# Two norm rows moved inside a fp32 encoder-block kernel: the memory's row into the next projection, and the first token half's norm in two parts

## The chip, the cores and the metric

The kernel runs on one core of one Trainium2 chip. The metric is device time in microseconds. The kernel before takes 880.38 us, the median of 3 runs (880.06 to 880.5).

The engines are called as in the profile: PE is the matrix engine (PEld its weight loads), DVE the vector engine, ACT the scalar engine, POOL the general one, and SP the queue that issues most transfers.

## The reference

One layer of a hybrid encoder block on 512 tokens of width 1024, in fp32, with 256 memory tokens:

```
h = rms_norm(x);  proj = h @ w_in          # mLSTM q,k,v,o,gates | NA q,k,v | memory q | merge gates
y_ml = bidirectional mLSTM(...)            # chunks of 64, 4 heads of 128
y_na = 2-D neighbourhood attention(...)    # 8 heads of 64, window 8 x 16
mem_k, mem_v = split(rms_norm(mem) @ w_mem_kv)
y_xa = cross attention(xa_q, mem_k, mem_v) # 4 heads of 128
merged = g_ml*(y_ml@w_br_ml) + g_na*(y_na@w_br_na) + g_xa*(y_xa@w_br_xa)
x = x + merged @ w_out
x = x + (gelu(conv3(a)) * u) @ w_down      # a, u = split(rms_norm(x) @ w_up), width 2816 each
return rms_norm(x)                         # y = x * rsqrt(mean(x*x) + eps) * g
```

Two of the four norms matter here: that of the memory, and the last one, over the finished x.

## The kernel before

**Layout.** Activations are kept transposed: 128 features on the partitions, the 512 tokens along the free axis, eight such tiles for a width of 1024. Each fp32 operand is split into a high and a low fp32r part, and each product is three fp32r matmuls (`mm3`, L213 to L215): high by high, high by low, low by high. Weights stream from memory; each block of 1024 columns is split on arrival by ACT (L195) and DVE (L196).

**Norms.** The gain is folded into the split, and the reciprocal root is applied to the product. It is needed in two shapes, a column (one value for each token, tokens on the partitions) and a row (the value of each token in every partition). Three helpers make them:

- `two_parts` (L294) splits the sum of squares over feature tiles into a high and a low fp32r tile, one ACT copy (L296) and one DVE subtraction (L297).
- `rstd_cols` (L300) sums over partitions with two fp32r matmuls against a matrix of ones (L305), picks the diagonal with a DVE reduction against the identity (L309, one for each 128 tokens, and a read of its accumulator), and raises to the power -0.5 on POOL (L312).
- `rstd_row` (L315) splits the column into high and low (ACT L319, DVE L320), multiplies the identity by each value (DVE L325, one for each 128 tokens and part) to get diagonals, spreads them with two fp32r matmuls against ones (L326), and copies the result out (ACT L328).

**Order.** Each engine works through its instructions in the order of the program; the tile framework adds the semaphore waits. A projection `proj` is 24 matmuls, and a caller can hang work between its steps with `at={k: f}`. A generator holds the mLSTM and attention work, and `step()` puts a piece of it between projections; `tc.issue_after` keeps an instruction behind a named one.

**The memory's norm.** The squares of the memory are summed during the projections for its queries. In the loop over the four "o" projections (L980 to L994) the column is made after f = 1 and the row after f = 2, as a whole: diagonals and matmuls one behind the other. The row is first read at L999, after the first key projection.

**The end of the kernel** (`last_tiles`, L1111). The last down projection adds to x. Tokens 0 to 255, the first half, are finished in the transposed layout: `half_tile` makes features 640 to 1023 for them in three tiles (`f` = 5, 6, 7), and adds their squares to the sum `acc3`. Then comes one more half tile, f = 5 for the second half of tokens. The first half's last norm is made under it: after its step 5 `cols_a` runs, two fp32 matmuls of one column (L1138), mean and eps on DVE (L1140), the power on POOL (`power`, L1108), and two diagonals on DVE (L1144); after its last step `row_a` runs, one fp32 matmul against ones (L1148) and an ACT copy (L1150). Then eight DVE multiplications (`scale_a`, L1154) scale the first half, and two transfers (`store_a`, L1157) write it out.

Tokens 256 to 511 are finished the other way round, in two rounds of 128 tokens (t = 2 and t = 3): tokens on the partitions, eleven steps `k` of three matmuls each, and between them transposes of finished features (`turn`, L1173). In round 2, at step 3 and at step 4, `sums` (L1174 to L1180) sums `acc3` over partitions for these tokens by a matmul (L1177) and scales on DVE (L1179). From the second of these a value for round 3 is worked out (L1197) and written into column 256 of round 3's own accumulator bank; the first matmul of round 3 waits for that write. At the end of each round come the square sum of its own 256 columns, a power, the scaling and the stores.

Of the kernel before, what the change touches and what calls it, by code (L numbers as in the profile page):

```python
# [11 lines left out]
F32 = mybir.dt.float32  # L12
F32R = mybir.dt.float32r
AF = mybir.ActivationFunctionType
ALU = mybir.AluOpType
AX = mybir.AxisListType

P = 128
# [92 lines left out]
def hybrid_block(ctx, tc, xg, xT, memT, wflat, vecs, gbias, nabias, outa, outb):  # L111
# [18 lines left out]
    def unit(dt=F32):  # L130
        return up.tile([P, UNIT], dt, tag="unit", name=nm("u"))
# [10 lines left out]
    def atps():  # L142
        return atp.tile([P, 512], F32, tag="at", name=nm("at"))
# [156 lines left out]
    def rstd_cols(parts, ntok, tag, n=D):  # L300

        nt = ntok // P
        ps = atps()
        for i in range(2):
            st["mm"] = PE.matmul(ps[:, :ntok], onesr, parts[i], start=i == 0, stop=i == 1).ins  # L305

        v, junk = tiny(nt), scr(P)
        for t in range(nt):
            V.tensor_tensor_reduce(junk, ps[:, t * P:(t + 1) * P], ident, 1.0 / n, EPS, ALU.mult, ALU.add,  # L309
                                   accum_out=v[:, t:t + 1])  # L310
        col = cp.tile([P, nt], F32, name=f"rc_{tag}")
        st["pool"] = G.tensor_tensor(col, v, nhalf[:, :nt], op=ALU.pow).ins  # L312
        return col

    def rstd_row(col, ntok, tag):  # L315

        nt = ntok // P
        ch, cl = tp.tile([P, 32], F32R, tag="tiny", name=nm("y"), bufs=12)[:, :nt], tiny(nt)
        A.activation(ch, col, AF.Copy)  # L319
        V.tensor_tensor(cl, col, ch.bitcast(F32), op=ALU.subtract)  # L320
        pb = atps()
        for n, c in enumerate((ch.bitcast(F32), cl)):
            dg = sp.tile([P, S], F32R, tag="scr", name=nm("s"))[:, :ntok]
            for t in range(nt):
                V.tensor_scalar(dg[:, t * P:(t + 1) * P], ident, c[:, t:t + 1], None, op0=ALU.mult)  # L325
            PE.matmul(pb[:, :ntok], onesr, dg, start=n == 0, stop=n == 1)  # L326
        rb = cp.tile([P, ntok], F32, name=f"rb_{tag}", tag=f"rb{ntok}", bufs=1)
        A.activation(rb, pb[:, :ntok], AF.Copy)  # L328
        return rb
# [42 lines left out]
    def proj(key, XHs, XLs, n=S, bank=None, at={}):  # L372
        ws = weights(key)
        ps = (bank or mmps)()
        for k in range(KT):
            mm3(ps[:, :n], ws[k][0], ws[k][1], XHs[k], XLs[k], k == 0, k == KT - 1)
            if k == 1:
                flush()
            if k in at:
                at[k]()  # L380
        return ps
# [576 lines left out]
    def step(n=1):  # L958
        quota[0] += n
        while quota[0] >= 1 and gens:  # L960
            try:
                next(gens[0])
                quota[0] -= 1
            except StopIteration:
                gens.pop(0)
        if not gens:
            quota[0] = 0.0
# [3 lines left out]
    gens.append(ml_all())  # L971

    xq = unit()
    for f in range(4):
        ps = proj(("xaq", f), XH, XL)
        V.tensor_tensor(xq[:, f * S:(f + 1) * S], ps, rb, op=ALU.mult)
        mem_part(f)
        step(RB)
    for f in range(4):
        ps = proj(("o", f), XH, XL)  # L980
        t = scr()
        V.tensor_tensor(t, ps, rb, op=ALU.mult)
        A.activation(t, t, AF.Tanh, scale=0.5)
        if f == 0:
            so.append(unit())
            msum = two_parts(macc, M)
        if f == 1:

            with tc.issue_after(st["mm"]):
                mrc = rstd_cols(msum, M, "m")  # L990
        if f == 2:
            mrb = rstd_row(mrc, M, "m")
        V.tensor_scalar(so[0][:, f * S:(f + 1) * S], t, 1.0, None, op0=ALU.add)
        step(RB)  # L994
    mkv = unit()
    mk, mv = mkv[:, 0:1024], mkv[:, 1024:2048]
    for f in range(4):
# [113 lines left out]
    def last_tiles(U, UL_):  # L1111
# [20 lines left out]
        for f in range(LF - 1, KT):  # L1132
            half_tile(f, slice(0, Hf))

        def cols_a():
            ps = atps()
            for t in range(2):
                PE.matmul(ps[:, t:t + 1], acc3[:, t * P:(t + 1) * P], ones[:, 0:1], start=True, stop=True)  # L1138
            v = tiny(2)
            V.tensor_scalar(v, ps[:, :2], 1.0 / D, EPS, op0=ALU.mult, op1=ALU.add)  # L1140
            col = power(v)
            half["d"] = scr(Hf)
            for t in range(2):
                V.tensor_scalar(half["d"][:, t * P:(t + 1) * P], ident, col[:, t:t + 1], None, op0=ALU.mult)  # L1144

        def row_a():
            pb = atps()
            PE.matmul(pb[:, :Hf], ones, half["d"], start=True, stop=True)  # L1148
            half["r"] = scr(Hf)
            A.activation(half["r"], pb[:, :Hf], AF.Copy)  # L1150

        def scale_a(eng, *tiles):
            for i in tiles:
# [2 lines left out]
        def store_a(i):  # L1156
            SY.dma_start(outa[i * P:(i + 4) * P, :].rearrange("(f p) s -> p f s", p=P), x2v[i // 4][:, :, :Hf])  # L1157

        half_tile(LF - 1, slice(Hf, S), {5: cols_a, HF - 1: row_a})
        for i in (0, 4):  # L1160
            scale_a(V, *range(i, i + 4))
            store_a(i)
        banks = [mmps(), mmps()]
        for t in range(2, NT):
            tsl, osl = slice(t * P, (t + 1) * P), slice((t - 2) * P, (t - 1) * P)
            last = t == NT - 1
            bank = banks[t - 2]
            ps = bank[:, :256]
            pts = [atps(), mmps()]
            r = scr(256)  # L1170

            def turn(i):
                PE.transpose(pts[i // 4][:, i % 4 * P:(i % 4 + 1) * P], x2[i][:, tsl], ident)  # L1173

            def sums(sl):
                pc = atps()
                PE.matmul(pc[:, :1], acc3[:, sl], ones[:, 0:1], start=True, stop=True)  # L1177
                v0 = tiny(1)
                V.tensor_scalar(v0, pc[:, :1], 1.0 / D, EPS, op0=ALU.mult, op1=ALU.add)  # L1179
                return v0  # L1180

            for k in range(HF):
                mm3(ps, U[k][:, tsl], UL_[k][:, tsl], ws[k][0], ws[k][1], k == 0, k == HF - 1)
                if k == 1 and last:

                    for i in range(LF, KT):
                        PE.matmul(ps[:, (i - LF) * P:(i - LF + 1) * P], x2[i][:, tsl], ident, start=False, stop=False)
                elif k == 1:
                    for i in range(LF, KT):
                        turn(i)  # L1190
                    A.activation(r, pts[1][:, 256:], AF.Copy)
                if not last and k == 3:
                    v0 = sums(tsl)
                if not last and k == 4:

                    v1 = sums(slice(S - P, S))
                    V.scalar_tensor_tensor(banks[1][:, 256:257], v1, D ** 0.5, power(v1), op0=ALU.mult, op1=ALU.mult)  # L1197
                if not last and k == HF - 3:
                    for i in range(LF):
                        turn(i)  # L1200
            if last:
                for i in range(LF):
                    turn(i)
            sq, v = scr(257), tiny(1)
            if last:
                oa, ob = scr(), scr()

                A.activation(sq, bank[:, :257], AF.Square, scale=D ** -0.5, accum_out=v)
                A.activation(oa[:, 256:], pts[0][:, 256:], AF.Copy)
                col = power(v)  # L1210
                A.activation(oa[:, :256], pts[0][:, :256], AF.Copy, scale=col)
                first = V.tensor_scalar(oa[:, 256:], oa[:, 256:], col, None, op0=ALU.mult).ins
                SY.dma_start(outb[osl, :512], oa)

                with tc.issue_after(first):
                    V.scalar_tensor_tensor(ob[:, 256:], ps, col, gfin, op0=ALU.mult, op1=ALU.mult)
                A.activation(ob[:, :256], pts[1][:, :256], AF.Copy, scale=col)
                A.dma_start(outb[osl, 512:], ob)
                continue
            V.tensor_tensor(r, ps, r, op=ALU.add)  # L1220
            ss = tiny(1)
            A.activation(sq[:, :256], r, AF.Square, accum_out=ss)
            V.tensor_scalar(v, ss, 1.0 / D, v0, op0=ALU.mult, op1=ALU.add)
            col = power(v)
            o = unit()
            V.scalar_tensor_tensor(o[:, 768:1024], r, col, gfin, op0=ALU.mult, op1=ALU.mult)
            SY.dma_start(outb[osl, 768:], o[:, 768:1024])
            A.activation(o[:, :512], pts[0], AF.Copy, scale=col)
            SY.dma_start(outb[osl, :512], o[:, :512])
            A.activation(o[:, 512:768], pts[1][:, :256], AF.Copy, scale=col)  # L1230
            SY.dma_start(outb[osl, 512:768], o[:, 512:768])
# [162 lines left out]
```

## Time and profile before

| | |
|---|---|
| median of 3 runs | 880.38 us (880.06 to 880.5) |
| the profiled execution's own time | 880.21 us |
| its span | 878.4 us |
| PE busy | 873.1 us, 99% of the span |
| DVE, ACT, POOL busy | 580.5, 453.4, 126.9 us |
| memory row made (L319 to L328) | from 135.5 to 140.0 us |
| last half tile and first half's norm | from 858.6 to 864.0 us |
| rounds t = 2 and t = 3 on PE | from 863.2 to 873.8 us |

A row of a timeline has the start in us, the length in us, the engine, the line, the operation, its output and input tiles with their shapes, how many instructions are merged into it, and in brackets how long the engine sat idle before and what ended that. The length of a matmul is the time until its result stands; the next one starts earlier, so the distance between starts is what one costs PE. A fp32 matmul (not fp32r) shows as two records.

### The profile page before, as it was taken

Reading aid. Unit: us, or ns where it says so; the run is one execution under the profiler, and the core shown is the slowest. Engines: PE = TensorE matmul, PEld = TensorE weight load, DVE = VectorE, ACT = ScalarE, POOL = GpSimd, SP = SyncE. Lnnn points to the kernel's source line nnn. Section 1 sums busy time; section 2 is a strip of 40 time slices with the busy share of each in tenths; the row PEclk is TensorE's granted clock in tenths of the full one; section 3 lists DMA queues with packets and bytes.
Section 4 is the critical chain, followed back from the end, with each engine's and each line's share of the span. In section 5 each row is a group of like instructions: output and inputs, shape, how many; then the busy total and the mean of one; then the engine's idle time right before and its main releaser. Section 6 shows DMA issues by size and latency. Waiting matters only on the chain.

```text
span 878.4 us, 12253 instructions
## 1 busy us (share of the span) xinstructions
PE 873.1 (99%) x4338; PEld 740.0 (84%) x4338; DVE 580.5 (66%) x1206; ACT 453.4 (52%) x955; POOL 126.9 (14%) x203
## 2 busy tenths in 40 slices
PE   9999999999999999999999999999999999999997
PEld 7898889888888888888888888888888888888897
DVE  7694687766577758898676558776633466666433
ACT  7363556654556658888544435444422344444532
POOL 0101100000072460700000002111100011111011
PEclk9999999999999999999999999999999999999999
DMA  7224643522242353533223422222233322222412
GB/s 274 99 73 145 203 133 121 169 93 87 84 121 87 107 159 118 156 110 130 97 97 109 144 107 94 99 97 96 74 101 104 107 96 98 97 98 85 141 34 96
DMA packets 39293, 99.68 MB, mean 113 GB/s; under 512 B 5688, under 2 KB 13752, under 8 KB 39232
## 3 DMA queue, kind: packets, MB, share of 16 engines
q1 hardware_dynamic: 31440, 92.19, 30.6%
q0 software_dynamic: 7360, 6.32, 3.2%
q8 instruction: 34, 0.56, 0.3%
q10 hardware_dynamic: 432, 0.39, 0.1%
q14 instruction: 27, 0.22, 0.1%
HBM read 94.67 MB, written 4.21 MB: 113 GB/s over the span
## 4 chain that ended last, share of the span: by engine, by line
PE 99%; issue 0%; ACT 0%; DVE 0%; POOLq 0%; POOL 0%; DVEq 0%
PE mm L215 29%; PE mm L213 29%; PE mm L214 29%; PE at L214 2%; PE at L213 2%; PE at L215 2%; PE at L832 1%; PE at L686 1%; PE at L813 1%; PE at L651 1%; PE at L688 1%; PE at L794 0%; PE at L795 0%; PE at L667 0%; PE at L920 0%
## 5 line engine op out<-in xcount | busy, mean ns | idle before, releaser
L213 PE MATMUL mm<-u,wh 128*128 128x512 f32 (+1 forms) x1076 | 416.8, 388 | 0.0
L215 PE MATMUL mm<-u,wl 128*128 128x512 f32 (+1 forms) x1076 | 413.6, 384 | 0.0
L214 PE MATMUL mm<-u,wh 128*128 128x512 f32 (+1 forms) x1076 | 413.4, 384 | 0.0
L195 ACT ACTIVATE wh<-wr 128x512 fp32r<-128x512 f32 (+3 forms) x299 | 185.2, 622 | 246.7 <-PE mm L214 193.3
L196 DVE TENSOR_TENSOR wl<-wr,wh 128x512 fp32r<-128x512 f32 (+3 forms) x300 | 202.9, 678 | 91.5 <-ACT wh L195 86.9
L215 PEld LDWEIGHTS mm<-u,wl 128*128 128x128 f32 x1076 | 202.2, 188 | 40.7 <-DVE wl L196 0.6
L214 PEld LDWEIGHTS mm<-u,wh 128*128 128x128 f32 x1076 | 202.4, 188 | 39.1 <-DVE u L220 0.3
L213 PEld LDWEIGHTS mm<-u,wh 128*128 128x128 f32 x1076 | 202.4, 188 | 38.6 <-ACT wh L195 0.3
L1263 POOL TENSOR_TENSOR s<-s,rb 128x512 f32<-128x512 f32 x22 | 38.3, 1739 | 250.0 <-DVE s L1262 241.9
L499 POOL DMA_DIRECT2D u<-nav_d x128 | 62.2, 518 | 64.3 <-PE at L832 22.5
L219 ACT ACTIVATE u<-s 128x512 fp32r<-128x512 f32 x26 | 16.4, 631 | 56.3 <-DVE s L1266 56.1
L1266 DVE TENSOR_TENSOR s<-mm,s 128x512 f32<-128x512 f32 x22 | 15.2, 691 | 25.1 <-POOL s L1263 25.1
L419 ACT ACTIVATE s<-pad,vec 128x512 f32<-128x512 f32 x30 | 24.4, 812 | 9.2 <-DVE pad L417 9.2
L420 DVE SCALAR_TENSOR_TENSOR s<-pad,vec,s 128x512 f32<-128x512 f32 x30 | 23.6, 785 | 5.9 <-ACT s L419 5.8
L220 DVE SCALAR_TENSOR_TENSOR u<-s,u 128x512 fp32r<-128x512 f32 x26 | 18.0, 691 | 14.3 <-ACT u L219 14.1
L1262 DVE SCALAR_TENSOR_TENSOR s<-s,s 128x512 f32<-128x512 f32 x22 | 15.2, 692 | 13.4 <-ACT s L1261 13.3
L312 POOL TENSOR_TENSOR rc<-y,nhalf 128x4 f32<-128x4 f32 x1 | 1.0, 1032 | 152.5 <-DVE y L309 152.5
L421 DVE SCALAR_TENSOR_TENSOR s<-pad,vec,s 128x512 f32<-128x512 f32 x30 | 22.5, 750 | 0.8
L1261 ACT ACTIVATE s<-s 128x512 f32<-128x512 f32 x22 | 13.9, 631 | 15.1 <-DVE s L1260 15.1
L417 DVE TENSOR_TENSOR pad<-mm,rb 128x512 f32<-128x512 f32 x22 | 15.1, 690 | 7.3 <-PE mm L215 6.6
L1045 DVE TENSOR_TENSOR s<-mm,rb_x 128x512 f32<-128x512 f32 x16 | 11.0, 688 | 12.6 <-PE mm L215 12.6
L213 PE MATMUL mm<-wh,u 128*128 128x512 f32 x48 | 19.0, 396 | 0.0
(301 smaller groups left out, 1030.7 us busy)
## 6 DMA issues: line engine op xcount, KB each, us to landing
wr<-wflat SPq DMA_DIRECT2D x141, 512.0 KB, 3.2
nab<-nabias SPq DMA_DIRECT2D x16, 256.0 KB, 2.6
u<-nav_d POOLq DMA_DIRECT2D x128, 32.0 KB, 2.7
s<-xT SPq DMA_DIRECT2D x15, 256.0 KB, 3.7
wr<-wflat SPq DMA_DIRECT2D x14, 192.0 KB, 2.3
nav_d<-nv POOLq DMA_DIRECT2D x8, 256.0 KB, 2.7
R<-rd SPq DMA_DIRECT2D x8, 256.0 KB, 3.8
wr<-wflat SPq DMA_DIRECT2D x2, 544.0 KB, 3.2
```

What stands on the lines that cost most here:

```text
L195: A.activation(h[:, u:v], src, AF.Copy)
L196: V.tensor_tensor(l[:, u:v], src, h[:, u:v].bitcast(F32), op=ALU.subtract)
L213: PE.matmul(ps, lh, rh, start=start, stop=False)
L214: PE.matmul(ps, lh, rl, start=False, stop=False)
L215: st["mm"] = PE.matmul(ps, ll, rh, start=False, stop=stop).ins
L219: A.activation(h, src, AF.Copy, scale=scale)
L220: V.scalar_tensor_tensor(l, src, scale, h.bitcast(F32), op0=ALU.mult, op1=ALU.subtract)
L419: A.activation(t1, pad[:, 0:512], AF.Identity, scale=vcol(w, i), bias=vcol(b, i))
L420: V.scalar_tensor_tensor(t1, pad[:, 1:513], vcol(w, n + i), t1, op0=ALU.mult, op1=ALU.add)
L421: V.scalar_tensor_tensor(t1, pad[:, 2:514], vcol(w, 2 * n + i), t1, op0=ALU.mult, op1=ALU.add)
L499: G.dma_start(vw[r * 32:(r + 1) * 32, i * 256:(i + 1) * 256], nav_v[hf, r, CW[b]:CW[b] + 32, hp * 256:(hp + 1) * 256])
L1263: G.tensor_tensor(c, c, rb2, op=ALU.mult)
```

## The change

1. `rstd_row` is cut in two. `row_parts` makes both diagonals; `rstd_row` then issues the two matmuls and the copy, from given diagonals or from those that it makes.
2. For the memory the diagonals are made where the whole row was made before, after the "o" projection f = 2. The two matmuls and the copy are issued within the next projection, f = 3, after its step 1.
3. For the first half of tokens the fp32 norm is replaced by the general helpers: `two_parts` of `acc3` ahead of the last half tile, `rstd_cols` and `row_parts` after its step 6 (before: step 5), and the row's matmuls and copy after step 2 of round t = 2 (before: after the half tile's last step). The eight scalings and the two stores go with the row, so they come after step 2 of round 2 too. So the second half tile's addition to x (L1126) stands behind `row_parts` on DVE, and the scalings stand behind the first scaling of `sums` and ahead of the second one on DVE.

```diff
-        col = cp.tile([P, nt], F32, name=f"rc_{tag}")
+        col = tiny(nt) if tag == "a" else cp.tile([P, nt], F32, name=f"rc_{tag}")
...
-    def rstd_row(col, ntok, tag):
+    def row_parts(col, ntok):
         nt = ntok // P
         ch, cl = tp.tile([P, 32], F32R, tag="tiny", name=nm("y"), bufs=12)[:, :nt], tiny(nt)
         A.activation(ch, col, AF.Copy)
         V.tensor_tensor(cl, col, ch.bitcast(F32), op=ALU.subtract)
-        pb = atps()
-        for n, c in enumerate((ch.bitcast(F32), cl)):
+        dgs = []
+        for c in (ch.bitcast(F32), cl):
             dg = sp.tile([P, S], F32R, tag="scr", name=nm("s"))[:, :ntok]
             for t in range(nt):
                 V.tensor_scalar(dg[:, t * P:(t + 1) * P], ident, c[:, t:t + 1], None, op0=ALU.mult)
+            dgs.append(dg)
+        return dgs
+
+    def rstd_row(col, ntok, tag, parts=None):
+        dgs = parts or row_parts(col, ntok)
+        pb = atps()
+        for n, dg in enumerate(dgs):
             PE.matmul(pb[:, :ntok], onesr, dg, start=n == 0, stop=n == 1)
...
-        ps = proj(("o", f), XH, XL)
+        def mem_row():
+            with tc.issue_after(st["mm"]):
+                mrbs.append(rstd_row(mrc, M, "m", mparts))
+
+        ps = proj(("o", f), XH, XL, at={1: mem_row} if f == 3 else {})
...
         if f == 2:
-            mrb = rstd_row(mrc, M, "m")
+            mparts = row_parts(mrc, M)
...
+        asum = two_parts(acc3[:, :Hf], Hf)
+
         def cols_a():
-            ps = atps()
-            for t in range(2):
-                PE.matmul(ps[:, t:t + 1], acc3[:, t * P:(t + 1) * P], ones[:, 0:1], start=True, stop=True)
-            v = tiny(2)
-            V.tensor_scalar(v, ps[:, :2], 1.0 / D, EPS, op0=ALU.mult, op1=ALU.add)
-            col = power(v)
-            half["d"] = scr(Hf)
-            for t in range(2):
-                V.tensor_scalar(half["d"][:, t * P:(t + 1) * P], ident, col[:, t:t + 1], None, op0=ALU.mult)
-
-        def row_a():
-            pb = atps()
-            PE.matmul(pb[:, :Hf], ones, half["d"], start=True, stop=True)
-            half["r"] = scr(Hf)
-            A.activation(half["r"], pb[:, :Hf], AF.Copy)
+            half["c"] = rstd_cols(asum, Hf, "a")
+            half["p"] = row_parts(half["c"], Hf)
...
-        half_tile(LF - 1, slice(Hf, S), {5: cols_a, HF - 1: row_a})
-        for i in (0, 4):
-            scale_a(V, *range(i, i + 4))
-            store_a(i)
+        half_tile(LF - 1, slice(Hf, S), {6: cols_a})
...
+                if not last and k == 2:
+                    with tc.issue_after(st["mm"]):
+                        half["r"] = rstd_row(half["c"], Hf, "a", half["p"])
+                    for i in (0, 4):
+                        scale_a(V, *range(i, i + 4))
+                        store_a(i)
                 if not last and k == 3:
                     v0 = sums(tsl)
```

More of the change, by code (lines that the diff above doesn't have):

```diff
@@ L973, in hybrid_block @@
     xq = unit()
+    mrbs = []
     for f in range(4):
@@ L991, in hybrid_block @@
         if f == 2:
-            mrb = rstd_row(mrc, M, "m")
+            mparts = row_parts(mrc, M)
         V.tensor_scalar(so[0][:, f * S:(f + 1) * S], t, 1.0, None, op0=ALU.add)
         step(RB)
+    mrb = mrbs[0]
     mkv = unit()
```

## The prediction

> **What bounds the kernel.** I read the clock row and the chain that ended last first, then the timelines of PE, DVE, ACT and POOL over the last 20 us, since both parts of the change lie in the order of a few instructions.
>
> ```profile
> PEclk9999999999999999999999999999999999999999
> ```
> ```profile
> PE 99%; issue 0%; ACT 0%; DVE 0%; POOLq 0%; POOL 0%; DVEq 0%
> ```
>
> PE is the chain from end to end, at full clock. So each change counts by what it puts on PE or takes off it, and by the time that PE waits. A microsecond of DVE or ACT counts only where PE waits for it. The profiled execution took 880.21 us, 0.17 us less than the median of 880.38; I work out differences against its trace and add them to the median.
>
> The end of the kernel on PE, then DVE, ACT, POOL and the store queue at the same time:
>
> ```profile
> 860.60 0.28 PE L215 MATMUL mm<-u,wl 128*128 128x256 f32 x1
> ...
> 861.28 0.28 PE L214 MATMUL mm<-u,wh 128*128 128x256 f32 x1
> ...
> 862.83 0.28 PE L215 MATMUL mm<-u,wl 128*128 128x256 f32 x1
> ...
> 863.50 0.28 PE L214 MATMUL mm<-u,u 128*128 128x256 f32 x1
> ...
> 865.02 0.30 PE L1177 MATMUL at<-ones,acc 128*128 128x1 f32 x2
> ...
> 868.64 0.28 PE L213 MATMUL mm<-u,u 128*128 128x256 f32 x1
> ```
> ```profile
> 863.15 0.42 DVE L1126 TENSOR_TENSOR u<-mm,u 128x256 f32<-128x256 f32 x1 [0.44 <-PE mm L215]
> 864.07 0.43 DVE L1154 TENSOR_TENSOR u<-u,s 128x256 f32<-128x256 f32 x1 [0.49 <-ACT s L1150]
> 864.41 0.42 DVE L1129 TENSOR_TENSOR acc<-acc,s 128x256 f32<-128x256 f32 x1
> 864.74 2.43 DVE L1154 TENSOR_TENSOR u<-u,s 128x256 f32<-128x256 f32 x7
> 867.09 0.21 DVE L1179 TENSOR_SCALAR y<-at 128x1 f32<-128x1 f32 x2
> 867.97 0.17 DVE L1197 SCALAR_TENSOR_TENSOR mm<-y,y 128x1 f32<-128x1 f32 x1 [0.66 <-POOL y L1108]
> ```
> ```profile
> 859.66 0.51 ACT L1130 ACTIVATE u<-u,vec 128x256 f32<-128x256 f32 x1
> 863.65 0.38 ACT L1150 ACTIVATE s<-at 128x256 f32<-128x256 f32 x1 [3.47 <-PE at L1148]
> 863.93 0.41 ACT L1128 ACTIVATE s<-u 128x256 f32<-128x256 f32 x1
> 864.37 0.51 ACT L1130 ACTIVATE u<-u,vec 128x256 f32<-128x256 f32 x1
> 864.79 0.36 ACT L1191 ACTIVATE s<-mm 128x256 f32<-128x256 f32 x1
> ```
> ```profile
> 861.49 0.70 POOL L1108 TENSOR_TENSOR y<-y,nhalf 128x2 f32<-128x2 f32 x1 [11.67 <-DVE y L1140]
> 867.38 0.55 POOL L1108 TENSOR_TENSOR y<-y,nhalf 128x1 f32<-128x1 f32 x1 [5.19 <-DVE y L1179]
> ```
> ```profile
> 865.90 1.80 SPq L1157 DMA_DIRECT2D outa<-u  x2
> 871.30 0.34 SPq L1227 DMA_DIRECT2D outb<-u  x1
> ```
>
> See three things. PE has no gap here. The sum of the second half (DVE L1129) ends at 864.83, just ahead of the matmul that reads it (865.02). And the write that round 3 waits for (L1197) ends at 868.14, only 0.50 ahead of round 3's first matmul (868.64). So DVE has little to spare at two places, and the change queues more work on DVE ahead of both.
>
> **The memory's row.** Moved are two fp32r matmuls and a copy; the ACT copy, the DVE subtraction and the four diagonals stay where they were. No transfer moves.
>
> ```profile
> 130.60 0.40 PE L305 MATMUL at<-s,onesr 128*128 128x256 f32 x2
> 130.84 0.39 PE L667 MATMUL at<-u,u 128*128 128x128 f32 x2
> ```
> ```profile
> 138.55 0.40 PE L214 MATMUL mm<-u,wh 128*128 128x512 f32 x1
> ...
> 139.38 0.40 PE L215 MATMUL mm<-u,wl 128*128 128x512 f32 x1
> ```
>
> Two matmuls of 256 columns cost 0.24 (130.60 to 130.84), 0.12 each. Between L214 and L215 from 138.55 on lie the row's two matmuls and, between them, one fp32 matmul of the mLSTM, of 128 columns (half of the 0.43 that one of 256 costs below, 0.22). From 0.83 go an ordinary step of 0.23 (two of 256 columns), the 0.24 and the 0.22: 0.14 is lost, to the wait for the diagonals and to changing between fp32 and fp32r. In the changed order the fp32 matmul stands with its like, and the row comes four matmuls later (0.9 us), behind its diagonals. I take -0.15, between 0.1 (the new place breaks up a stream of fp32r) and -0.25. The row is first read after the first key projection; a copy that is a microsecond later meets nobody.
>
> **The last norm: PE's work.** Removed are the one-column fp32 sums and the fp32 row: 861.28 less 860.60 is 0.68, where two ordinary steps take 0.24, so 0.44; 863.50 less 862.83 is 0.67, so 0.43. Added are four fp32r matmuls of 256 columns, 0.48. Net -0.39. Two of the last four transposes now stand ahead of round 3 (0.22); at the end they saved nothing, as ACT waited for the last sum there, not for them.
>
> **The last norm: PE's first wait.** All DVE work up to the diagonals now stands ahead of the addition L1126, and L1126 leads to the sum that PE reads at step 3 of round 2. The helper's rows, from the norms of x, whose form is the same for twice the tokens:
>
> ```profile
> 28.25 0.61 PE L305 MATMUL at<-s,onesr 128*128 128x512 f32 x2
> ```
> ```profile
> 29.45 0.29 DVE L309 CUSTOM_DVE_ANT_0 s<-at,ident 128x128 f32<-128x128 f32 x1 [1.23 <-PE at L305]
> ```
> ```profile
> 30.83 1.03 POOL L312 TENSOR_TENSOR rc_x<-y,nhalf 128x4 f32<-128x4 f32 x1 [28.29 <-DVE y L309]
> ```
> ```profile
> 132.33 0.88 POOL L312 TENSOR_TENSOR rc_m<-y,nhalf 128x2 f32<-128x2 f32 x1 [17.42 <-DVE y L309]
> ```
> ```profile
> 523.74 0.21 ACT L319 ACTIVATE y<-rc 128x4 fp32r<-128x4 f32 x1 [2.42 <-POOL rc L312]
> ```
> ```profile
> 523.98 0.16 DVE L320 TENSOR_TENSOR y<-rc,y 128x4 f32<-128x4 f32 x1 [1.39 <-ACT y L319]
> 524.06 1.26 DVE L325 TENSOR_SCALAR s<-ident,y 128x128 fp32r<-128x128 f32 x6
> ```
>
> - Split of `acc3`: ACT is free at 860.15 (859.66 + 0.51), copy 0.38 and subtraction 0.42 with handoffs of 0.04: ready at 861.0. PE: without the old sums, step 6 runs from 860.72 to 861.08 and the two sums start at 861.08 and 861.20. Nothing waits; the last result stands at 861.48 (0.28 long).
> - Reduction: four tiles took 1.38 from first start to POOL, so two take 0.71 (0.33 each and the handoff). Its start: the row of x shows 0.59 from PE's last result (28.86) to 29.45 with DVE idle. All other handoffs from PE to an idle DVE are near 0.04 (862.83 + 0.28 to 863.15). I take 0.04, since that one was the first use of the instruction and had a separate wait in front of it, and keep 0.59 as the other end: 861.52, POOL at 862.23.
> - Power of two columns: 0.70 with DVE idle, 0.88 with DVE busy; DVE is idle here, so 0.70: 862.93. High and low part: ACT and DVE, 0.24 to the subtraction and 0.08 to the first diagonal: 863.26. Diagonals start 0.20 apart: the high pair is ready at 863.74, the low one at 864.13.
> - PE: round 2 starts at 862.76, two steps, two transposes (0.22), step 2 until 864.06. The row's matmuls then find their diagonals and end at 864.30. Step 3 ends at 864.66.
> - L1126 follows the diagonals on DVE, at 864.04 instead of 863.15, though its input stood at about 862.9. Then 0.42 and 0.04, ACT's square 0.41 and 0.04, DVE's addition 0.42: 865.37. PE's sum follows at 865.45: it waits 0.76 from 864.66.
>
> **PE's second wait.** On ACT the square (864.50), L1191's copy, the scaling and the row's copy follow each other at the old distances: 864.94, 865.24, 865.66, ended 866.04. The eight scalings start at 866.08, 0.336 apart (864.74 to 867.09 for seven), and end at 868.77. Only then come the second scaling of `sums`, POOL and the write: 0.99 from the start of that scaling (867.15) to the end of the write (868.14). So the write ends at 869.76, and round 3 starts at 869.80. PE itself would be there at 865.45 + 3.62 (865.02 to 868.64) + 0.22 for the two transposes, 869.29; it waits another 0.51.
>
> Here a page speaks for more. The Trainium skill, "VectorE: DVE Perf Modes", section "The DRAIN you can't avoid", says that the next vector instruction does not start until the pipe is empty; eight scalings of 0.43 would then take 3.44 and put the total 0.75 higher, near 882.1. The row of these very instructions, at this size, shows starts 0.336 apart, so the row decides and the rule gets no chance of its own.
>
> The two stores move with the scalings, by some 1.6 to 2 us on SP: the next store in that queue is issued at 871.30, so their cover is over 3 us and they cost nothing; without it they would cost what they are late.
>
> **Sum.** Round 3 starts at 869.80 instead of 868.64: +1.16. (By parts: waits 0.76 and 0.51, transposes 0.22, work -0.39, together 1.10; the rest is rounding.) Round 3 and what follows it are unchanged, and the other work of round 2's end, later by as much, has over 1 us before ACT is needed again. With the memory's -0.15 it is +1.0: 881.4 us.
>
> **Rivals.**
> 1. The reduction starts late (0.59), perhaps with the slow power (0.88) too: the whole chain moves by 0.55 to 0.73, and both waits with it: 881.9 to 882.2.
> 2. No wait binds, because the framework's order or shorter handoffs let L1126 and the write through in time: only work counts, -0.39 and -0.15: 879.8. Against it: on DVE L1126 stands in program order behind the diagonals, and the scalings ahead of the write. If only the second wait is covered, +0.76 - 0.39 - 0.15, 880.6.
> 3. Slower for certain: PE's clock steps down in the new waits. Round 3 has 33 matmuls at 0.12; at half clock 4.0 us more: 885.4. It decides from about a fifth of round 3 (0.8 us lost). For it: two new idle stretches where there was none. Against it: they are half a microsecond and 0.8 us long. The Trainium skill, "TensorE: Matmul & The Clock Gate", section "Part 1: The HAM clock gate", lets the clock halve after an idle window of about 3.4 us; the trace has no idle stretch of PE inside the kernel that could test it.
> 4. The memory's row does not do what it says: 0 instead of -0.15, inside every range.
>
> **How the numbers follow.** About 0.2%, 1.76 us, is what a measurement of this kernel can tell from no change; slower means above 882.1, faster below 878.6. The forecast (both waits, quick start) has 0.62, with its own range of 880.9 to 882.0; rival 1 has 0.17, rival 2 has 0.10 for none and 0.06 for one wait, rival 3 0.03; 0.02 is left. Half of rival 1, all of rival 3 and a tail of the forecast are above the bound: 0.20 slower. Faster needs more than all the work removed: 0.02. The range leaves out rival 2's lowest case, rival 3 and the tails: 880.4 to 882.3.
>
> **What would show it.** In the profile after: idle time of PE ahead of the sum of round 2's step 3, ended by the addition to `acc3`, 0.76; and ahead of round 3's first matmul, ended by the write to its bank, 0.51; L1126's successor at about 864.0 and eight scalings from about 866.1; the reduction 0.04 or 0.59 behind its matmul; around 139 us the two row matmuls side by side. Wrong would be: no idle PE there, or a late reduction, or a clock row below 9 in the last slice.

## The result, and the profile after

The changed kernel takes 881.51 us (median of 21 runs, 881.23 to 882.34). The kernel before, run beside it, takes 880.45 us (21 runs, 880.06 to 881.39). The ratio is 1.0012, with a 95% interval of 1.0006 to 1.0017: slower by about 1.06 us. The interval excludes no change: these runs tell a difference of 0.12%, although the prediction took 0.2% as the least that can be told. The forecast was 881.4.

The page of the changed kernel: the clock that was granted in each slice, and the chain that ended last, by engine.

```profile
PEclk9999999999999999999999999999999999999999
...
PE 98%; DVE 1%; issue 1%; POOL 0%; ACT 0%; POOLq 0%
```

The clock row is the same. The chain is not: before it was PE alone, now DVE and "issue" hold 1% each. The chain of the changed kernel in order of time (start, length, what) names the pieces. It leaves PE behind the two reduction matmuls of the half tile:

```profile
861.53 0.28 PE at L305 x2
861.83 0.29 DVE s L309
...
862.54 0.71 POOL y L312
...
863.67 0.79 DVE s L325 x4
864.46 0.34 DVE u L1140
...
864.82 0.43 ACT s L1142
865.27 0.44 DVE acc L1143
865.71 0.14 issue
865.85 0.37 PE at L1178 x2
...
866.39 2.68 DVE u L1158 x8
...
869.81 0.17 DVE mm L1205
```

This is the path that the prediction described: reduction, power, four diagonals, the addition to x (L1140, which was L1126), the square, the addition to `acc3` (L1143, was L1129), PE's sum (L1178, was L1177), the eight scalings (L1158, was L1154), and the write (L1205, was L1197) that round 3 waits for. PE's rows in the same stretch, from the timeline, with the issue of SP's last store at the end:

```profile
858.85 0.28 PE L213 MATMUL mm<-u,wh 128*128 128x256 f32 x1
...
864.34 0.56 PE L334 MATMUL at<-s,onesr 128*128 128x256 f32 x2
864.74 0.28 PE L213 MATMUL mm<-u,u 128*128 128x256 f32 x1
864.98 0.28 PE L215 MATMUL mm<-u,u 128*128 128x256 f32 x1
865.85 0.35 PE L1178 MATMUL at<-ones,acc 128*128 128x1 f32 x2 [0.59 <-DVE acc L1143]
866.06 0.36 PE L213 MATMUL mm<-u,u 128*128 128x256 f32 x1
866.50 0.28 PE L1178 MATMUL at<-ones,acc 128*128 128x1 f32 x2
866.64 0.36 PE L213 MATMUL mm<-u,u 128*128 128x256 f32 x1
...
868.57 0.38 PE L1174 MATMUL mm<-ident,u 128*128 128x128 f32 x2
868.71 0.36 PE L213 MATMUL mm<-u,u 128*128 128x256 f32 x1
868.91 0.28 PE L214 MATMUL mm<-u,u 128*128 128x256 f32 x1
...
869.51 0.38 PE L1174 MATMUL at<-ident,u 128*128 128x128 f32 x2
870.03 0.19 PEld L213 LDWEIGHTS mm<-u,u 128*128 128x128 f32 x1 [0.38 <-DVE mm L1205]
870.03 0.39 PE L213 MATMUL mm<-u,u 128*128 128x256 f32 x1
870.26 0.28 PE L214 MATMUL mm<-u,u 128*128 128x256 f32 x1
...
876.34 0.33 SPq L1221 DMA_DIRECT2D outb<-s  x1
```

Read the distances between starts, since the brackets of PE's own rows count only from the modelled end of the matmul before:

- 864.34 to 864.74 is 0.40, where two row matmuls need 0.24. PE waited 0.16 for the diagonals.
- 864.98 to 865.85 is 0.87 instead of 0.12: the first wait, 0.75.
- 865.85 to 866.06 is 0.21, where the same sum later takes 0.14 (866.50 to 866.64): 0.07 more, right behind a wait.
- 869.51 to 870.03 is 0.52 for a fp32 transpose (two records). At 868.57 the same transpose takes 0.14, and the matmul behind it 0.20 instead of 0.12: 0.22 for it in all. So the second wait is 0.52 - 0.14 = 0.38, as PEld's row says in its bracket.
- 870.03 to 870.26 is 0.23, where behind a transpose 0.20 is usual: 0.03 more.

The ruler for what follows is the **stretch** from the first matmul of the last half tile to the issue of SP's last store (the very last store, on ACT's queue, is issued 0.37 later in both kernels). The expectations below count to the end of the span instead, which is 878.4 - 858.55 = 19.85 before and 879.9 - 858.85 = 21.05 after. After, the stretch is 876.34 - 858.85 = 17.49 us. The same rows before:

```profile
858.55 0.28 PE L213 MATMUL mm<-u,wh 128*128 128x256 f32 x1
...
874.86 0.33 SPq L1213 DMA_DIRECT2D outb<-s  x1
```

That is 874.86 - 858.55 = 16.31, so the last stage costs 1.18 us more. The memory's row gives a little back. From the reduction L305 to the mLSTM matmul behind the projection f = 3 (L675, which was L667) the changed kernel takes 144.71 - 131.00 = 13.71 us. Its rows, and those of before:

```profile
131.00 0.40 PE L305 MATMUL at<-s,onesr 128*128 128x256 f32 x2
...
140.36 0.40 PE L334 MATMUL at<-s,onesr 128*128 128x256 f32 x2
...
144.71 0.38 PE L675 MATMUL at<-u,u 128*128 128x128 f32 x2
```
```profile
144.38 0.38 PE L667 MATMUL at<-u,u 128*128 128x128 f32 x2
```

Before, it was 144.38 - 130.60 = 13.78. The row's two matmuls now stand side by side (x2, 140.36), and the gain is 0.07 here. (The ten profiles with the row moved show 13.68 to 13.71, the two with it in one piece 13.78 and 13.80, so it is about 0.1.) So the trace says 1.18 - 0.07 = +1.11, and the medians say +1.06.

### The profile page after: what moved, and what is told of

The parts are those of the page before. It is cut to its first block, busy times and chain, and to the rows that moved or that the text cites. A ratio compares the mean times of both kernels' runs of the same rounds, so it can differ in the third digit from the quotient of the medians.

```text
span 879.9 us, 12257 instructions
## 1 busy us (share of the span) xinstructions
PE 873.6 (99%) x4336; PEld 740.5 (84%) x4336; DVE 581.8 (66%) x1213; ACT 453.6 (52%) x957; POOL 127.0 (14%) x203
## 4 chain that ended last, share of the span: by engine, by line
PE 98%; DVE 1%; issue 1%; POOL 0%; ACT 0%; POOLq 0%
PE mm L213 29%; PE mm L215 29%; PE mm L214 29%; PE at L214 2%; PE at L213 2%; PE at L215 2%; PE at L840 1%; PE at L694 1%; PE at L821 1%; PE at L659 1%; PE at L696 1%; PE at L802 0%; PE at L803 0%; PE at L675 0%; PE at L928 0%
```

## The experiments

My theory was that the last norm costs two waits of PE, each caused by an instruction that stands behind others in DVE's queue, and that each goes when that order is changed. The rivals were that PE's own work, the later stores, the memory's row or a slow restart carry the difference.

**The memory's row alone.** The last norm is as before; only the memory's row is cut in two.

```diff
-        half_tile(LF - 1, slice(Hf, S), {6: cols_a})
+        half_tile(LF - 1, slice(Hf, S), {5: cols_a, HF - 1: row_a})
+        for i in (0, 4):
+            scale_a(V, *range(i, i + 4))
+            store_a(i)
```

> The kernel before with the memory's row alone moved into the next projection. Theory: PE's row matmuls side by side, 0.12 us less between the same two steps of the projection, 880.3 us, not to be told from the kernel before by its time. Rival (the new place costs, by breaking up a stream of fp32r matmuls or a late row): 880.5 to 880.8 us, and a longer distance between the same steps.

Measured: 880.44 us (11 runs) against 880.44, ratio 0.9999 (0.9990 to 1.0008); the memory's stretch 144.72 - 131.03 = 13.69. So the cost is not here. A gain of 0.09 is read from the trace alone; the times can't show it.

**The last norm alone.** The memory's row is in one piece again.

```diff
-        ps = proj(("o", f), XH, XL, at={1: mem_row} if f == 3 else {})
+        ps = proj(("o", f), XH, XL)
...
-            mparts = row_parts(mrc, M)
+            mrbs.append(rstd_row(mrc, M, "m"))
```

> Only the last norm of the first half changed; the memory's row is made in one piece, as before. Theory (both waits are the last norm's, and the memory's row is worth 0.08): from the first matmul of the last half tile to the end +1.20 us against the kernel before (21.05), the waits ahead of the sum and of round 3 as in the changed kernel, total about 881.6. Rival (the memory's row, moved, costs something that the profiles hide): 880.5 or less.

Measured: 881.93 us (11 runs) against 880.54, ratio 1.0016 (1.0007 to 1.0025). The stretch is 876.50 - 859.02 = 17.48, as with both parts (17.49). The last norm carries the loss.

**The additions first.** `st["dg"]` is the last diagonal. The second half's addition to x goes ahead of the split of the column and of the diagonals on DVE; the addition to `acc3` comes behind the diagonals.

```diff
-            V.tensor_tensor(xf, ps, xf, op=ALU.add)
+            add = V.tensor_tensor(xf, ps, xf, op=ALU.add).ins
+            if at:
+                with tc.issue_after(add):
+                    half["p"] = row_parts(half["c"], Hf)
+                add = st["dg"]
...
-            V.tensor_tensor(acc3[:, cs], acc3[:, cs], sq, op=ALU.add)
+            with tc.issue_after(add):
+                V.tensor_tensor(acc3[:, cs], acc3[:, cs], sq, op=ALU.add)
...
             half["c"] = rstd_cols(asum, Hf, "a")
-            half["p"] = row_parts(half["c"], Hf)
```

> The changed kernel with one order turned round on DVE: the second half tile's addition to x stands ahead of the split column and the diagonals, its addition to the sum of squares behind them. Theory (two waits, both by order on DVE): PE waits for the first round-2 sum 0 to 0.2 us instead of 0.75; the row's copy on ACT, the scalings and the write for round 3 come about 0.85 earlier too, so the second wait stays at 0.3 to 0.5; in all 0.85 less than the changed kernel, about 880.6 us. Rival (the second wait takes it up, because the write for round 3 hangs on something else than the first delay): the first wait goes, the second grows by as much, 881.4 us. Rival (no wait matters, PE has more work): 881.5 us.

Measured: 880.94 us (11 runs) against 880.44, ratio 1.0007 (0.9998 to 1.0016). Its timeline:

```profile
864.29 0.63 PE L334 MATMUL at<-s,onesr 128*128 128x256 f32 x2
864.76 0.29 PE L213 MATMUL mm<-u,u 128*128 128x256 f32 x1
865.13 0.28 PE L1182 MATMUL at<-ones,acc 128*128 128x1 f32 x2
...
864.40 0.42 DVE L1148 TENSOR_TENSOR acc<-acc,s 128x256 f32<-128x256 f32 x1
```

The addition to `acc3` now ends at 864.82, and the sum starts 0.37 after the step's first matmul (three steps of 0.12), without a wait. The stretch is 875.54 - 858.80 = 16.74: 0.75 shorter than after, where 0.85 was expected. The wait for the write is still there, since the write still stands behind the scalings. The row's matmuls wait 0.23 now (864.29 to 864.76 is 0.47), as the addition stands ahead of their diagonals.

**The write first.** The eight scalings and the two stores go behind the write; nothing else is changed.

```diff
                         half["r"] = rstd_row(half["c"], Hf, "a", half["p"])
-                    for i in (0, 4):
-                        scale_a(V, *range(i, i + 4))
-                        store_a(i)
...
                     V.scalar_tensor_tensor(banks[1][:, 256:257], v1, D ** 0.5, power(v1), op0=ALU.mult, op1=ALU.mult)
+                    for i in (0, 4):
+                        scale_a(V, *range(i, i + 4))
+                        store_a(i)
```

> The changed kernel with the eight scalings and the two stores moved behind the second sum of round 2, so that the write for round 3 stands behind two scalings instead of eight. Theory: the first wait stays at 0.75; the second one (0.3 to 0.4 with the slow restart behind it) goes, about 0.5 to 0.6 less than the changed kernel, 880.9 to 881.0 us. Rival (the later stores push the last stores, which is what costs): the first half's stores start no earlier than in the changed kernel, so no gain, 881.5 us or more. Rival (another wait in its place: the addition of round 2 now stands behind the scalings, so its power, scaling and stores are late): round 3's own end is late, 881.3 us or more.

Measured: 881.01 us (11 runs), ratio 1.0007 (0.9998 to 1.0015). Its timeline:

```profile
866.28 0.35 PE L1178 MATMUL at<-ones,acc 128*128 128x1 f32 x2 [0.59 <-DVE acc L1143]
...
868.18 0.17 DVE L1202 SCALAR_TENSOR_TENSOR mm<-y,y 128x1 f32<-128x1 f32 x1 [0.45 <-POOL y L1122]
...
870.30 0.28 PE L213 MATMUL mm<-u,u 128*128 128x256 f32 x1
...
869.09 1.73 SPq L1161 DMA_DIRECT2D outa<-u  x2
```

The first wait is as it was (0.59 in the bracket) and the second is gone: the write ends at 868.35, and round 3 starts at 870.30, without a gap. The stretch is 876.15 - 859.28 = 16.87, or 0.62 shorter. The framework, which chooses the order of an engine's instructions where nothing ties it, now leaves the transpose behind round 3, so this 0.62 is the transpose (0.22), the wait (0.38) and the slow step (0.03) together. The stores are issued at 869.09, later than in the changed kernel (867.81), and cost nothing: that rival falls.

**Both.** The two edits together.

> Both orders turned round, as in e3_addition_first and e4_write_first. Theory: what is left is PE's smaller work, -0.39, and the memory's row, -0.12: 879.9 to 880.0 us, 0.4 to 0.5 under the kernel before, with no wait of PE over 0.2 us in the last 20 us. Rival (the waits are not additive, a third one shows): between 880.3 and 881.0 us.

Measured: 880.28 us (11 runs) against 880.44, ratio 1.0000 (0.9991 to 1.0009). The stretch is 874.74 - 858.62 = 16.12, shorter than after by 1.37 = 0.75 + 0.62. The two waits are additive. Against before, however, it is 0.19 shorter, not the 0.39 that was expected:

```profile
864.12 0.63 PE L334 MATMUL at<-s,onesr 128*128 128x256 f32 x2
864.59 0.28 PE L213 MATMUL mm<-u,u 128*128 128x256 f32 x1
```

0.47 for two matmuls of 0.12 each: the row still waits 0.23 for its diagonals. No list of waits shows this, because PE counts as busy until the modelled end of the matmul before.

**More work ahead of the write.** Three DVE multiplications into a tile that nobody reads stand ahead of the second scaling of `sums`. They are added work; nothing is left out.

```diff
+                    extra = scr(Hf)
+                    for i in range(3):
+                        more = V.tensor_tensor(extra, x2[i][:, :Hf], half["r"], op=ALU.mult).ins
...
+                    with tc.issue_after(more):
                         V.tensor_scalar(v1, pc[:, :1], 1.0 / D, EPS, op0=ALU.mult, op1=ALU.add)
```

> The changed kernel, with three more DVE multiplications of a 128x256 tile placed ahead of the second scaling of the sums, and so ahead of the write that round 3 waits for. Their result is not used. Theory (round 3 waits for that write, which stands behind DVE's queue): three additions of some 0.34 us, and round 2's addition to r which the framework puts among them, so the write ends about 1.7 us later, round 3 starts about 1.7 us later, total about 883.2. Rival (round 3 is late for PE's own work or a slow restart, and the write has slack): 881.5 to 881.9.

Measured: 884.03 us (5 runs) against 880.54, ratio 1.0039 (1.0026 to 1.0052). PE in the timeline:

```profile
872.37 0.39 PE L213 MATMUL mm<-u,u 128*128 128x256 f32 x1 [1.55 <-DVE mm L1212]
872.60 0.28 PE L214 MATMUL mm<-u,u 128*128 128x256 f32 x1
```

The stretch is 878.68 - 859.31 = 19.37: 1.88 longer than after, where the theory had 1.7, and every bit of it is in front of round 3, ended by the write. The write has no slack. (The framework also put two more transposes, 0.44, ahead of round 3 here; they fall into the wait.) The time is 0.8 us above the 883.2 expected: 0.18 of that is in the stretch (1.88 for 1.7), and the profiled run had reached the last half tile 0.46 later than the changed kernel's (859.31 against 858.85), ahead of every edited instruction; such starts differ from run to run (below). The rest is within the spread of five runs.

**The row a step later.** "Both", with the row's two matmuls behind step 3 instead of step 2.

```diff
-                if not last and k == 2:
+                if not last and k == 3:
                     with tc.issue_after(st["mm"]):
                         half["r"] = rstd_row(half["c"], Hf, "a", half["p"])
```

> The changed kernel with both additions and the write ahead in DVE's order, and the row's two matmuls behind step 3 of round 2 instead of step 2. Theory (what is left of PE idle after the two waits is 0.23 us at the row's matmuls, which wait for their diagonals): that wait goes, from the first matmul of the last half tile to the end -0.40 us against the kernel before (19.45), total about 879.9 to 880.0, faster than both kernels. Rival (a row that comes later makes the scalings, or what follows them, late): 880.3 or more, with a new wait.

Measured: 880.25 us (11 runs) against 880.54, ratio 0.9996 (0.9988 to 1.0005).

```profile
864.24 0.42 DVE L1148 TENSOR_TENSOR acc<-acc,s 128x256 f32<-128x256 f32 x1
...
864.48 0.40 PE L334 MATMUL at<-s,onesr 128*128 128x256 f32 x2
864.80 0.35 PE L1182 MATMUL at<-ones,acc 128*128 128x1 f32 x2
865.02 0.36 PE L213 MATMUL mm<-u,u 128*128 128x256 f32 x1
```

The stretch is 874.66 - 858.63 = 16.03: 0.28 under before, 0.09 better than "both" and not the whole 0.23. From the row to the sum it is 0.32 instead of 0.24, and the sum takes 0.22 instead of 0.14: 0.16 lost. Either the sum still waited for the addition to `acc3`, which ended at 864.66, or changing from fp32r to fp32 costs that much here.

**The sums a step later too.** This tells the two apart: the same matmuls, with the sums behind steps 4 and 5.

```diff
                 if not last and k == 3:
                     with tc.issue_after(st["mm"]):
                         half["r"] = rstd_row(half["c"], Hf, "a", half["p"])
-                    v0 = sums(tsl)
-                if not last and k == 4:
+                if not last and k == 4:
+                    v0 = sums(tsl)
+                if not last and k == 5:
                     v1 = sums(slice(S - P, S))
```

> The kernel of e7 (row behind step 3), with the two sums of round 2 a step later as well, behind steps 4 and 5. Theory (in e7 the first sum still waits, by about 0.1 to 0.15 us, for the second half's addition, which ends just behind it): no wait of PE is left, so from the first matmul of the last half tile to the end -0.40 us against the kernel before (19.45), 0.12 less than e7's 19.57; total about 880.0. Rival (e7's loss is the change between fp32r and fp32 matmuls, and not a wait): 19.57 as in e7.

Measured: 879.92 us (11 runs) against 880.39, ratio 0.9995 (0.9986 to 1.0004).

```profile
858.54 0.28 PE L213 MATMUL mm<-u,wh 128*128 128x256 f32 x1
...
864.38 0.40 PE L334 MATMUL at<-s,onesr 128*128 128x256 f32 x2
864.62 0.29 PE L213 MATMUL mm<-u,u 128*128 128x256 f32 x1
...
864.98 0.28 PE L1182 MATMUL at<-ones,acc 128*128 128x1 f32 x2
865.11 0.36 PE L213 MATMUL mm<-u,u 128*128 128x256 f32 x1
...
874.42 0.33 SPq L1224 DMA_DIRECT2D outb<-s  x1
```

The row takes 0.24, the sum 0.13, and the stretch is 15.88: 0.43 under before, and 0.15 under the version with only the row moved. It was a wait. To tell 0.5 us from nothing, the same kernel was timed twice more.

> The kernel of e8 unchanged, timed again. Theory (PE's saved work of 0.39 to 0.43 us in the last stage and 0.08 us at the memory's row are the whole difference): about 0.5 us, 0.05%, under the kernel before. Rival (no difference): the medians agree within 0.2 us.

> The kernel of e8 once more, so that the difference of 0.05% can be told from none; the same expectation: 0.5 us under the kernel before, or within 0.2 us of it.

Measured: 880.01 and 880.21 us (11 runs each) against 880.63, ratios 0.9993 (0.9984 to 1.0002) and 0.9992 (0.9983 to 1.0001). Each interval by itself just includes no change. All three medians are lower by 0.42 to 0.62, and the 33 runs together have a median of 880.01, against 880.51 for the 36 runs of before. Resampling these runs gives 0.27 to 0.67 for the difference of the two medians (95% of the draws), so all together do tell it from none. It is the 0.5 us that the trace gives (0.43 in the stretch and 13.78 - 13.70 = 0.08 at the memory's row), and it is 0.06%: with its waits taken away the change saves what it removes on PE, and no more.

## Why the prediction was right, point by point

The ledger of the last stage, with the kernel without waits (15.88) as its base, which is 0.43 under before:

| | predicted | measured | read from |
|---|---|---|---|
| PE's work | -0.39 | -0.43 | stretch without waits against before |
| row's matmuls wait for their diagonals | 0 | 0.16 | 864.34 to 864.74 |
| first wait | 0.76 | 0.75 | 864.98 to 865.85 |
| slow step behind it | 0 | 0.07 | 865.85 to 866.06 |
| transpose ahead of round 3 | 0.22 | 0.22 | 868.57 to 868.91, less a step |
| second wait | 0.51 | 0.38 | PEld's row at 870.03 |
| slow step behind it | 0 | 0.03 | 870.03 to 870.26 |
| sum | +1.10 | +1.18 | stretch 17.49 against 16.31 |
| memory's row | -0.15 | -0.07 | 13.71 against 13.78 |

- **PE is the bound, and only its waits and its work count.** Right. The stores that came later cost nothing, and DVE's and ACT's added work is on the path only where PE waits for it.
- **The reduction starts 0.04 behind its matmul, not 0.59 (rival 1).** Right: it starts 0.02 behind the modelled end (861.81 to 861.83 in the chain). The power took 0.70, as in the row with DVE idle.
- **The first wait.** Place, cause and size were right, and moving the additions showed it: -0.75. (By my own times its size is 865.45 - 864.66 = 0.79, not the 0.76 that I wrote.) One handoff in it was mis-sized: from the addition to the sum I took 0.08, and the chain shows 0.14 of issue. That the row's own wait (0.16) had already delayed PE by then shortened this one to 0.75.
- **"The row's matmuls then find their diagonals."** Wrong. By my times the row's matmuls would have started at 864.06 and the low diagonals, which only the second of them reads, were ready at 864.13, 0.05 ahead of its start (864.18); I read that as no wait, and the handoff from DVE to PE was left out. It measured 0.16, and 0.23 once the addition to x stood ahead of the diagonals.
- **The second wait.** The mechanism was right (the write stands behind eight scalings), shown by taking it away (-0.62 with the transpose and the slow step) and by making it longer (+1.88). The size was 0.38, not 0.51. Counted from the first matmul of the half tile, the write ended at 11.13 us (869.81 + 0.17 - 858.85), where I had 11.21, and round 3 started at 11.18 (870.03 - 858.85), where I had 11.25: 0.07 of the difference. The other 0.06 is PE, which came later: at 10.80 (869.51 + 0.14 - 858.85), where I had 10.74. The first sum was 0.10 later (7.00, where I had 6.90), and from there to the wait it took 3.80 instead of 3.84, since the slow step of 0.08 that is part of the transpose's 0.22 falls behind the wait. And what I called two transposes is one, with two records; its 0.22 was right.
- **The work.** -0.39 was near: -0.43.
- **The memory's row.** -0.15 was too much; 0.07 (about 0.1 over all profiles), inside the range as I wrote it (0.1 to -0.25). The row lost 0.14 among the mLSTM's matmuls, and some of that came back in steps of 0.23 to 0.24 around the new place.
- **The scalings' distance.** Eight took 2.76 us (866.31, the group on DVE), that is 0.334 from start to start, against 0.42 for one:

```profile
866.31 2.76 DVE L1158 TENSOR_TENSOR u<-u,rb_a 128x256 f32<-128x256 f32 x8
```

  The Trainium skill, "VectorE: DVE Perf Modes", section "The DRAIN you can't avoid", has each instruction wait until the one before has left the pipe, and adds that a next one that is not held back starts earlier. I took only the first of these; this row agrees with the second.
- **The clock (rival 3).** It did not step down in the waits; the clock row is full up to the end of PE's work, and even the wait of more than 1.5 us ahead of round 3 in the kernel with more work left it at full.

So the total came out within 0.1 us partly by luck. In the sum of the parts, 1.10 where 1.18 was measured, the second wait was too long by 0.13, the work saved 0.04 more, and three small losses of PE (0.16, 0.07, 0.03) were missing. The forecast of 881.4 did not use that sum, but the start of round 3 on the time line, +1.16. The 0.06 between the two is not rounding: 0.03 is the first wait (0.79, not 0.76), and 0.03 is PE, which reached the first sum at 864.66 on that time line, where 865.02 less 0.39 is 864.63. Errors cancelled in the 1.16 too. Round 3 started only 1.09 later (11.18 behind the first matmul of the half tile, against 10.09 before), and "round 3 and what follows it are unchanged" was wrong by 0.09: from its first matmul to SP's last store it took 6.31 instead of 6.22, because its first step, now behind a transpose and a wait, took 0.23 instead of 0.12. The two large waits were right in place and cause; the sum was better than its terms.

## What to carry to other kernels

Moving work to an engine with time to spare costs nothing only if nothing that the busy engine needs soon stands behind it in that queue: here an addition and a one-column write, both short, were held by diagonals and scalings that could have waited. Where two waits follow each other, the second is shortened by whatever delays the first, so work out the whole time line and not each wait by itself; and when one wait is removed, look for the next one by the distances between starts, since short waits on PE are not listed. Compare such small changes in a stretch of the trace: the same kernel, profiled three times, reached the last half tile at 858.54, 858.91 and 859.17, but its last stretch was 15.88, 15.87 and 15.88.

## What the runs showed of the hardware that was not expected

- **What fp32 among fp32r costs shows in the step behind it.** A fp32 transpose of 128 columns takes 0.14 to the next start, and the fp32r matmul behind it 0.20 instead of 0.12, without any wait (868.57, 868.71, 868.91). Behind the second wait that step takes 0.23, and the same behind the wait of over 1.5 us (872.37 to 872.60): between these two it did not grow with the wait.
- **A sum that had to wait is slower itself.** Behind the first wait the one-column fp32 sum took 0.21 to the next start instead of 0.14, and 0.22 in the version with the row a step later, where the wait was only 0.08. It is not the wait alone: in the kernel before, the first of the two sums took 0.17 (865.02 to 865.19) without a wait. Why is open.
- **The handoff to PE differs.** From the addition on DVE to the sum on PE, which loads the new data as its weights, the chain shows 0.14 of issue; from PE to DVE and from ACT to DVE about 0.02 (861.53 + 0.28 to 861.83, 864.82 + 0.43 to 865.27). A load of new weights is not needed for it: the second of the row's matmuls, which streams the new diagonals against ones, starts 0.16 behind the last of them (863.67 + 0.79 = 864.46 to 864.74 - 0.12 = 864.62). Behind the write, round 3 starts after only 0.05 (869.98 to 870.03), with 0.03 more in its first step. Why these differ is open.
- **The clock falls at the end of the kernel, after different idle times.** PE's last matmul in the changed kernel ends at about 875.11, and the granted clock (0.75, the number behind POOL's busy time) falls to a half in the middle of this quarter of a microsecond:

```profile
877.00:877.25 0.25, 0.00 (x0) 0.00 (x0) 0.00 (x0) 0.00 (x0) 0.00 (x0) 0.75 0.20 82
```

  That is 2.0 us of idle time. In the kernel before, by the same view, the fall is at 878.86, 5.0 us behind the last matmul (873.84) and already behind the end of the span. In the twelve profiles of this case it came 2.0 to 5.2 us behind the last matmul, in three of them only at or behind the end of the span. This costs nothing here, as PE's work is done. The Trainium skill, "TensorE: Matmul & The Clock Gate", section "Part 1: The HAM clock gate", has the clock halve after an idle window of about 3.4 us that runs freely; the scatter, 3.2 us in all, agrees with a window that does not start with the idle time, but 2.0 us is less than one whole idle window.
